# Scores of 32 queries at a time with the 288 keys they see, instead of 128 queries with 384

## The chip, the cores and the metric

One Trainium2 chip; the program runs on one of its cores. The time is what one execution takes on the device, in microseconds (us). A core has TensorE (PE; its weight loads are shown as PEld), VectorE (DVE), ScalarE (ACT), GpSimd (POOL) and a sync engine (SP) whose queue issues nearly all transfers here. Each engine works through its own instructions in order and waits for others by semaphores. Matmuls read SBUF, the on-chip memory of 128 partitions, and write PSUM, the accumulators.

## What is computed

One encoder layer over 4096 tokens of width 1024:

```python
proj = rmsnorm(x) @ w_in                      # q | k | v | g_a | u_p | g_p
s = q @ k.T * scale + bias                    # 8 query heads, 2 key heads of 64
s = where(abs(i - j) <= 128 and 0 <= j < 4096, s, -1e30)
m = max(max(s), sink)
p = exp(s - m) / (sum(exp(s - m)) + exp(sink - m))
a = (p @ v) * silu(g_a)
mixed = concat([a, pool(u_p) * silu(g_p)]) @ w_out
x = x + rmsnorm(mixed)
```

A query sees the keys at most 128 tokens away. For a block of 128 queries these lie in three blocks of keys, 384; for 32 queries in a row they lie in 128 + 32 + 128 = 288.

## The kernel before

Every float32 operand that goes through TensorE is held as a pair of float16 numbers, a high part and the rest, and a product of two is three matmuls (high x high, rest x high, high x rest).

The kernel has two parts. Up to about 498 us it prepares the weights and computes the gates and the pooling branch. After that comes the attention part, on which the change bears. It goes through 32 blocks of 128 queries from block 31 down to block 0, and each block in two halves of the heads (half 0 and half 1, four heads each). One such half block is a *visit*. Between the visits TensorE projects keys, values and queries of later blocks (`project_t`, `proj_v`; `aq`, `kv` in the profile) and multiplies finished blocks with the output weights (`product`, `last_product`; `m`, `ms`, `z`).

What follows for each visit, with the lines of the listing:

- `scores` (L1423): two PSUM tiles `s`, each for two heads. The two key heads lie in the upper and lower 64 partitions, so the matmuls of a pair use the upper and lower 64 rows of the array (64x128 each). A pair streams 384 keys; three pairs per tile for the float16 parts, 12 matmuls a visit. The keys lie in a ring of 1024 columns (`k_all`), and where the window goes over its end (blocks 7, 8, 15, 16, 23 and 24) each matmul is cut in two, 24 a visit.
- `logits` (L1444): one VectorE instruction a head adds the bias (with -1e30 where a key is masked) and takes the maximum, from PSUM to the float32 tile `p`. GpSimd writes the sink beside it (L1438).
- `exps` (L1455, ScalarE, in place, with the sum), `denominators` (L1462, L1465, VectorE), `probs` (L1477, ScalarE, high parts to `pn`), `rests` (L1485, VectorE, the rest to `pn`).
- `turn` (L1494): one transpose by DMA on SP's queue brings `pn`, queries on partitions, to `pt`, keys on partitions: 2 parts x 4 heads x 3 key blocks, 3072 columns.
- later, `values` (L1565): 36 matmuls for both halves of a block, the value heads in the left and right 64 columns of the array; then `gate` (L1573) on VectorE.

Blocks 31 and 0 are at the ends of the sequence and see only two key blocks: 256 columns in place of 384, and a transpose of 2048 columns.

The order of work on each engine is written out by hand. Every step is entered with a due time (`due(t, fn, ...)`; `visit`, `do_q`, `do_kv`, `attend` and the `mix_` functions set them), the list is sorted by these, and each engine executes its instructions in this order; the due times are no clock, only an order. After block 2 the steps to the end are listed one by one (`at_`, with `soft` for a softmax).

PSUM tiles `s` have two buffers, which is one visit; `p` and `pn` have two, `pt` three.

Of the kernel before, what the change touches and what calls it, by code (L numbers as in the profile page):

```python
# [17 lines left out]
P = 128  # L18
# [9 lines left out]
PN_BUFS = 2  # L28
# [40 lines left out]
def hybrid_layer(ctx: ExitStack, tc, io, out):  # L69
# [32 lines left out]
    bias = yflat[:, : NH * 3 * P].rearrange("p (h k) -> p h k", h=NH)  # L102
# [49 lines left out]
    with ExitStack() as actx:  # L152
# [423 lines left out]
        def small_loads():  # L576
            row_t["sk"] = pa1.tile([P, NH], F32, name="sk")
            nc.sync.dma_start(
                row_t["sk"], io["sink"].rearrange("(o a) -> o a", o=1).to_broadcast([P, NH])
            )  # L580
            nc.sync.dma_start(psc, io["pool_scale"])
            row_t["m"] = pa1.tile([P, 3 * P], F32, name="mask")
            nc.sync.dma_start(row_t["m"], io["mask"])

        def bias_load():

            f0 = f_scr[0:1, 0, :]
            for p0 in range(0, P, FR):
# [3 lines left out]
                        tensor=f0.tensor, offset=f0.offset + P - 1 - p0,  # L592
                        ap=[[NF - 1, FR], [(FR + 1) * NF, NH], [1, 3 * P]],
# [770 lines left out]
    k_all = pb1.tile([P, 2, RK], F16, name="k_all")  # L1364
    q_t, v_t = {}, {}
# [26 lines left out]
    pt, p_t, s_t, nm_t, den_t, rd_t, pn_t = {}, {}, {}, {}, {}, {}, {}  # L1392
# [12 lines left out]

    def scores(b, half):
        u, tl = divmod(b, 2)
        tl *= P
        kbs = keys(b)
        nk = len(kbs) * P  # L1410
        k0 = (b - 1 + kbs[0]) * P % RK
        cut = min(nk, RK - k0)
        segs = [(0, cut, k0)] + ([(cut, nk, 0)] if cut < nk else [])
        s_t[b, half] = []
        for jj in range(2):
# [3 lines left out]
            for n, (qi, ki) in enumerate(((0, 0), (1, 0), (0, 1))):  # L1419
                for c0, c1, kc in segs:  # L1420
                    for gg in range(2):
                        a = slice(64 * gg, 64 * gg + 64)
                        nc.tensor.matmul(  # L1423
                            s_ps[:, gg, c0:c1], q_t[u, half][a, qi, jj, tl : tl + P],
                            k_all[a, ki, kc : kc + c1 - c0], start=(n == 0 and c0 == 0),
                            stop=(n == 2 and c1 == nk), skip_group_check=True,
                        )

    def logits(b, half, i):

        kbs = keys(b)
        nk, lo, j0 = len(kbs) * P, kbs[0] * P, 2 * half
        if i == 0:
# [3 lines left out]
            p = p_t[b, half] = pb.tile([P, 4, 3 * P + 1], F32, name=f"p{b}_{half}", tag="p")  # L1437
            nc.gpsimd.tensor_copy(  # L1438
                p.rearrange("p (g j) k -> p g j k", g=2)[:, :, :, nk],
# [4 lines left out]
        nc.vector.tensor_tensor_reduce(  # L1444
            out=p_t[b, half][:, hh, :nk], in0=s_t[b, half][jj][:, gg, :nk],
            in1=bias[:, h, lo : lo + nk], scale=negc[:, h : h + 1], scalar=nsink[:, h : h + 1],
            op0=ALU.add, op1=ALU.min, accum_out=nm_t[b, half][:, hh : hh + 1],
        )

    def exps(b, half, i):  # L1450
        nk = len(keys(b)) * P
# [4 lines left out]
            p[:, hh, : nk + 1], p[:, hh, : nk + 1], AF.Exp, bias=nm_t[b, half][:, hh : hh + 1],  # L1456
# [9 lines left out]

    def prob_view(b, half):
        nk = len(keys(b)) * P
        return pn_t[b, half][:, : 8 * nk].rearrange("p (v h k) -> p v h k", v=2, h=4)

    def probs(b, half, i):
        nk = len(keys(b)) * P
        if i == 0:
            pn_t[b, half] = pb.tile(
                [P, 2 * 4 * 3 * P], F16, name=f"pn{b}_{half}", tag="pn", bufs=PN_BUFS
            )
        nc.scalar.activation(  # L1477
            prob_view(b, half)[:, 0, i], p_t[b, half][:, i, :nk], AF.Copy,
# [3 lines left out]
    def rests(b, half, i):  # L1482
        nk = len(keys(b)) * P
        pn4 = prob_view(b, half)
        nc.vector.scalar_tensor_tensor(  # L1485
            out=pn4[:, 1, i], in0=p_t[b, half][:, i, :nk], scalar=rd_t[b, half][:, i : i + 1],
# [3 lines left out]
    def turn(b, half):  # L1490
        kbs = keys(b)
        t = pb.tile([P, 2 * 4 * 3, P], F16, name=f"pt{b}_{half}", tag="pt", bufs=PT_BUFS)
        t4 = t[:, : 8 * len(kbs), :]
        nc.sync.dma_start(t4, pn_t[b, half][:, : 8 * len(kbs) * P], transpose=True)  # L1494
# [622 lines left out]
```

## Time and profile before

| | |
|---|---|
| median of 3 runs | 1189.21 us (1188.63 to 1189.54) |
| the profiled execution | 1190.11 us |
| span of its instructions | 1188.3 us |
| granted TensorE clock, mean | 0.999 of full speed |
| busy: TensorE, VectorE, ScalarE, GpSimd | 97%, 78%, 61%, 23% of the span |
| busy share of the 16 DMA engines by queue 1 | 71.2% |
| DMA packets | 304567, of which 213776 under 512 B |

The profile is of one execution. A row of a timeline reads: start, duration, engine, line, operation, what it writes and reads with the number of partitions and elements, how many in a row, and in brackets the idle time of the engine just before and what ended it. A row of grouped instructions has the busy time and the mean duration of one in ns, then the idle time before them. A row of the waits has who waited for whom, the total in us, how often, and the longest. A matmul's recorded duration goes beyond the time for which the array is taken, so records of successive matmuls overlap.

The costliest groups of the attention part that bear on the change (a program-wide count each):

| | instructions | busy us | mean ns |
|---|---|---|---|
| scores, PE L1423 | 912 | 73.1 | 296 |
| values, PE L1565 | 1128 | 68.1 | 274 |
| logits, DVE L1444 | 256 | 156.0 | 666 |
| rests, DVE L1485 | 256 | 156.7 | 659 |
| exps, ACT L1455 | 256 | 153.0 | 599 |
| probs, ACT L1477 | 256 | 136.3 | 596 |
| transposes pt, SP L1494 | 64 | | 6.1 us from issue to landing |

### The profile page before, as it was taken

To read this page: it belongs to the slowest core of one execution; us is meant where nothing else is said; L and a number is where in the kernel's file an instruction comes from. 1 tells how busy PE (TensorE), PEld (TensorE's weight loads), DVE (VectorE), ACT (ScalarE), POOL (GpSimd) and SP (SyncE) were. 2 spreads that over 40 slices of the span, in tenths; PEclk is the share of its full clock that TensorE was granted. 3 is DMA by queue.
4 is the path that set the end of the run, shared out by engine and by line. 5 is a ranking of instruction groups with operands and counts; after the bars stand their busy time and mean duration, and the time that the engine had idled before them with its cause. 6 is when DMAs were issued, how large, how long until landed. Compare 5 with 4: busy or idle time off the path is not lost. (4 is left out here: it accounts for less than half of the span.)

```text
span 1188.3 us, 25535 instructions
## 1 busy us (share of the span) xinstructions
PE 1156.1 (97%) x10180; PEld 848.3 (71%) x10180; DVE 930.4 (78%) x1780; ACT 719.3 (61%) x1593; POOL 271.5 (23%) x281
## 2 busy tenths in 40 slices
PE   5999999999999999899999999999999999999997
PEld 4548888888888888766576676666666657657643
DVE  5787887688888876767777877787787787787786
ACT  5756666557566443366575666667666566656672
POOL 1000000000000000012433532533443443353231
PEclk9999999999999999999999999999999999999999
DMA  9578796959788547788786676786576577566694
GB/s 258 148 239 241 197 269 149 320 119 305 156 292 193 163 164 204 255 236 209 194 196 125 188 196 151 169 200 172 143 204 178 120 201 195 127 189 161 145 251 124
DMA packets 304567, 230.08 MB, mean 194 GB/s; under 512 B 213776, under 2 KB 270736, under 8 KB 299456
## 3 DMA queue, kind: packets, MB, share of 16 engines
q1 hardware_dynamic: 304448, 228.45, 71.2%
q8 instruction: 79, 1.29, 0.4%
q14 instruction: 40, 0.33, 0.1%
HBM read 115.14 MB, written 62.44 MB: 149 GB/s over the span
## 5 line engine op out<-in xcount | busy, mean ns | idle before, releaser
L935 PEld LDWEIGHTS <-wa 128*128 128x128 f16 x3360 | 328.2, 98 | 41.8 <-issue 3.2
L935 PE MATMUL ch<-xt,wa 128*128 128x256 f16 x1920 | 212.3, 273 | 1.0 <-DVE u L960 1.0
L1386 PEld LDWEIGHTS <-raw 128*128 128x128 f16 x1920 | 185.2, 98 | 33.8 <-issue 9.7
L1455 ACT ACTIVATE p<-p,nm 128x385 f32<-128x385 f32 (+1 forms) x256 | 153.0, 599 | 57.1 <-POOL p L1438 37.9
L1485 DVE SCALAR_TENSOR_TENSOR pn<-p,rd,pn 128x384 f16<-128x384 f32 (+1 forms) x256 | 156.7, 659 | 26.0 <-ACT pn L1477 25.4
L1386 PE MATMUL aq<-xt,raw 128*128 128x256 f16 x1536 | 173.1, 273 | 0.0
L1697 PE MATMUL ms<-wo,ys 128*128 128x512 f16 x720 | 162.8, 379 | 1.6 <-ACT pn L1477 1.6
L1444 DVE CUSTOM_DVE_ANT_0 p<-s,ybig,nsink 128x384 f32<-128x384 f32 (+1 forms) x256 | 156.0, 666 | 1.3 <-PE s L1423 1.0
L1477 ACT ACTIVATE pn<-p,rd 128x384 f16<-128x384 f32 (+1 forms) x256 | 136.3, 596 | 23.6 <-ACT p L1455 22.1
L1697 PEld LDWEIGHTS <-ys 128*128 128x128 f16 x720 | 68.9, 98 | 84.7 <-issue 4.2
L1697 PE MATMUL m<-wo,y 128*128 128x512 f16 x540 | 119.7, 380 | 0.7 <-POOL y L1603 0.5
L935 PE MATMUL cl<-xt,wa 128*128 128x256 f16 x960 | 106.9, 273 | 1.8 <-DVE cbig L960 1.0
L1697 PEld LDWEIGHTS <-y 128*128 128x128 f16 x540 | 51.4, 98 | 65.5 <-issue 4.5
L296 DVE TENSOR_TENSOR xt<-ybig,xt 128x1024 f16<-128x1024 f32 x56 | 67.7, 1221 | 22.8 <-ACT xt L291 22.5
L1733 POOL TENSOR_TENSOR mo<-mo,ybig 128x512 f32<-128x512 f32 x39 | 64.9, 1665 | 87.0 <-ACT jkb L1722 85.8
L204 POOL TENSOR_SCALAR ssq<-ssq 128x4 f32<-128x4 f32 (+1 forms) x11 | 3.6, 329 | 345.8 <-ACT jk L195 339.7
L1462 DVE TENSOR_SCALAR den<-den 128x4 f32<-128x4 f32 x64 | 17.4, 272 | 76.6 <-ACT p L1455 76.5
L1423 PE MATMUL s<-k_all,q 64*128 64x384 f16 (+2 forms) x912 | 73.1, 296 | 2.8 <-ACT q L1376 1.4
L1565 PE MATMUL o<-pt,vv 128*64 128x256 f16 x1128 | 68.1, 274 | 1.8 <-DMA pt<-pn 1.8
L1565 PEld LDWEIGHTS <-vv 128*64 128x64 f16 x1128 | 59.1, 110 | 8.1 <-issue 6.7
L1423 PEld LDWEIGHTS <-q 64*128 64x128 f16 x912 | 36.9, 94 | 36.1 <-issue 12.6
L291 ACT CAST xt<-ybig 128x1024 f16<-128x1024 f32 x56 | 57.1, 1041 | 4.0 <-PE cl L935 2.1
(184 smaller groups left out, 1652.6 us busy)
## 6 DMA issues: line engine op xcount, KB each, us to landing
x_scr<-xt SPq DMA_DIRECT2D x16, 1024.0 KB, 4.4
xt<-x_scr SPq DMA_DIRECT2D x15, 1024.0 KB, 7.7
xn<-in_x SPq DMA_DIRECT2D x28, 512.0 KB, 7.5
ybig<-in_xT SPq DMA_DIRECT2D x28, 512.0 KB, 6.7
xr<-in_x SPq DMA_DIRECT2D x28, 512.0 KB, 4.0
out<-xr SPq DMA_DIRECT2D x28, 512.0 KB, 3.6
yp_scr<-yt SPq DMA_DIRECT2D x32, 256.0 KB, 2.6
raw<-in_w_out SPq DMA_DIRECT2D x16, 512.0 KB, 7.9
```

What stands on the lines that cost most here:

```text
L291: nc.scalar.copy(couple(m, c)[:, w, 0], y_view(i))
L296: eng.tensor_tensor(out=o[:, w, 1], in0=y_view(i), in1=o[:, w, 0], op=ALU.subtract)
L935: nc.tensor.matmul(acc[:, c], wa[:, q, wi, slot * HK + k, c * P : (c + 1) * P], x[:, xi, k, :], start=(fresh and n == 0), stop=(n > 3 * 2 ...
L1386: nc.tensor.matmul(acc, w[:, j, k, :], x[:, k // HK, a, k % HK, :], start=(n == 0), stop=(n == 3 * KT - 1),)
L1423: nc.tensor.matmul(s_ps[:, gg, c0:c1], q_t[u, half][a, qi, jj, tl : tl + P], k_all[a, ki, kc : kc + c1 - c0], start=(n == 0 and c0 == 0), ...
L1444: nc.vector.tensor_tensor_reduce(out=p_t[b, half][:, hh, :nk], in0=s_t[b, half][jj][:, gg, :nk], in1=bias[:, h, lo : lo + nk], scale=negc[ ...
L1455: nc.scalar.activation(p[:, hh, : nk + 1], p[:, hh, : nk + 1], AF.Exp, bias=nm_t[b, half][:, hh : hh + 1], scale=-1.0, accum_out=den_t[b, ...
L1477: nc.scalar.activation(prob_view(b, half)[:, 0, i], p_t[b, half][:, i, :nk], AF.Copy, scale=rd_t[b, half][:, i : i + 1],)
L1485: nc.vector.scalar_tensor_tensor(out=pn4[:, 1, i], in0=p_t[b, half][:, i, :nk], scalar=rd_t[b, half][:, i : i + 1], in1=pn4[:, 0, i], op0= ...
L1565: nc.tensor.matmul(o_ps[a, 2 * half : 2 * half + 2], v[:, vi, kt, a], pt[b, half][:, pi, g, :, i, :], start=(n == 0), stop=(n == last),)
L1697: nc.tensor.matmul(z_t[u, tag], y[:, k, yi, :], wo[o][:, wi, k, :], start=(n == 0 and acc is None), stop=(n == 3 * HK - 1), skip_group_che ...
L1733: eng.tensor_tensor(out=mo, in0=mo, in1=gpost[:, cs], op=ALU.mult)
```

## The change

Each group of 32 queries is scored with the 288 keys that it sees. The 128 queries of a block become four groups, each on 32 columns of the array: with the two key heads in the two row halves, eight tiles of 64x32. The group r reads the keys from column 32 r of the window on, and its scores stand in the same 288 columns of PSUM on its 32 partitions; bias and mask are laid out in the same way. The softmax instructions then go over 288 columns (289 with the sink) in place of 384.

```diff
+QR = 32
+NK = 2 * P + QR
+MG = 3 * P - NK
+BIG = 1e30
...
+    pn = [pb1.tile([P, MG + 8 * 3 * P], F16, name=f"pn{i}") for i in range(2)]
...
+    def seen(b, r):
+
+        return (P - QR * r if b == 0 else 0), (2 * P - QR * r if b == NB - 1 else NK)
...
             for n, (qi, ki) in enumerate(((0, 0), (1, 0), (0, 1))):
-                for c0, c1, kc in segs:
-                    for gg in range(2):
...
+                for r in range(P // QR):
+                    lo, hi = seen(b, r)
+                    k0 = ((b - 1) * P + QR * r + lo) % RK
+                    cut = min(hi, lo + RK - k0)
+                    rows = slice(QR * r, QR * r + QR)
+                    for c0, c1, kc in ((lo, cut, k0), (cut, hi, 0)):
+                        for gg in range(2 * (c1 > c0)):
+                            a = slice(64 * gg, 64 * gg + 64)
+                            nc.tensor.matmul(
+                                s_ps[rows, gg, c0:c1],
+                                q_t[u, half][a, qi, jj, tl + QR * r : tl + QR * r + QR],
+                                k_all[a, ki, kc : kc + c1 - c0], start=(n == 0 and c0 == lo),
+                                stop=(n == 2 and c1 == hi), skip_group_check=True,
+                            )
```

That makes 48 matmuls a visit in place of 12, and 96 in place of 24 where the ring wraps; each comes with its weight load. In all 3648 in place of 912.

In blocks 31 and 0 the groups see different columns (256, 224, 192 and 160 of them), so each head's logits are four VectorE instructions of 32 partitions; GpSimd first fills `p` with 1e30, which the exponential turns to zero:

```diff
+            if edge_block:
+                nc.gpsimd.memset(p[:, :, :NK], BIG)
...
+        for r in range(P // QR if edge_block else 1):
+            rows = slice(QR * r, QR * r + QR) if edge_block else slice(0, P)
+            lo, hi = seen(b, r)
+            nc.vector.tensor_tensor_reduce(
+                out=p_t[b, half][rows, hh, lo:hi], in0=s_t[b, half][jj][rows, gg, lo:hi],
...
```

The probabilities of a group stand 32 r columns further left than before. `pn` is now two fixed tiles, one for each half, in which every 288 columns are followed by 96 zeros, with 96 more zeros ahead of all (`margins`, GpSimd, once at the start). The transpose of a half block becomes four, one for each group of 32 queries, and each begins 32 r columns further left, so that `pt` has the same layout as before:

```diff
     def turn(b, half):
...
+        for r in range(P // QR):
+            c0 = MG - QR * r
+            nc.sync.dma_start(
+                t[:, :, QR * r : QR * r + QR],
+                pn[half][QR * r : QR * r + QR, c0 : c0 + 8 * 3 * P], transpose=True,
+            )
```

Blocks 31 and 0 now also transpose all three key blocks (3072 columns); `values` reads the two that exist. The due times of all steps stay; the order on each engine differs by the added instructions alone, and the values' first weight load and matmul of each half wait for the four transposes where one matmul waited for one.

More of the change, by code (lines that the diff above doesn't have):

```diff
@@ L1419, in scores @@
             for n, (qi, ki) in enumerate(((0, 0), (1, 0), (0, 1))):
-                for c0, c1, kc in segs:
-                    for gg in range(2):
[L1422 to L1427, printed above, removed]
+                for r in range(P // QR):
[12 more added lines that the diff above has]
+                            )
     def logits(b, half, i):
-        kbs = keys(b)
-        nk, lo, j0 = len(kbs) * P, kbs[0] * P, 2 * half
+        j0 = 2 * half
+        edge_block = b in (0, NB - 1)
         if i == 0:
```

63 lines of the change are left out of this document (26 added, 37 removed).

## The prediction

> **What bounds the kernel now.** I read the page first, then the busy time by stretches, then TensorE's waits.
>
> ```profile
> span 1188.3 us, 25535 instructions
> ...
> PE 1156.1 (97%) x10180; PEld 848.3 (71%) x10180; DVE 930.4 (78%) x1780; ACT 719.3 (61%) x1593; POOL 271.5 (23%) x281
> ```
> ```profile
> core 0: us, PE busy (x) PEld busy (x) DVE busy (x) ACT busy (x) POOL busy (x), PEclk, DMA share, GB/s
> 498.00:540.00 42.00, 37.90 (x380) 28.06 (x381) 27.78 (x77) 26.49 (x70) 4.66 (x7) 1.00 0.84 239
> 540.00:1118.00 578.00, 576.44 (x5175) 384.70 (x5174) 453.17 (x1009) 365.71 (x916) 234.05 (x228) 1.00 0.70 174
> 1118.00:1170.00 52.00, 51.01 (x346) 26.71 (x344) 46.09 (x107) 33.43 (x88) 14.55 (x16) 1.00 0.81 208
> ```
> ```profile
> PE o L1565 <- DMA pt<-pn: 1.8, 2, 1.1
> PE ms L1697 <- ACT pn L1477: 1.6, 1, 1.6
> PE s L1423 <- ACT q L1376: 1.4, 2, 0.8
> PE s L1423 <- DVE q L1377: 0.9, 2, 0.4
> ```
>
> The windows give busy time and instructions of each engine per stretch. The attention part starts at about 498 us. From 540 to 1118 TensorE (PE) is busy 576.44 of 578 us: every nanosecond taken from a matmul group there is a nanosecond of the kernel, and VectorE (453.17) and ScalarE (365.71) have room. The other two stretches differ. From 1118 to 1170 VectorE is busy 46.09 of 52 us, nearly as tight as TensorE. And around 498 to 540 TensorE waited for q (1.4 and 0.9 us), that is for the two engines that split the projection; a later VectorE shows there at once. So the middle is priced by matmuls, the ends by VectorE's chain.
>
> **The scores in the middle.** A visit (one block of 128 queries, one half of the heads) has 12 matmuls now, 24 where the ring of keys wraps (blocks 7, 8, 15, 16, 23, 24). The change makes 48, and 96 at a wrap; each brings its weight load.
>
> ```profile
> 840.08 1.16 PE L1423 MATMUL s<-k_all,q 64*128 64x256 f16 x24
> ...
> 851.64 1.15 PE L1423 MATMUL s<-k_all,q 64*128 64x384 f16 x12
> ...
> 858.09 2.15 PE L1565 MATMUL o<-pt,vv 128*64 128x256 f16 x36
> ```
> ```profile
> L1423 PE MATMUL s<-k_all,q 64*128 64x384 f16 x576 | 55.3, 324 | 0.5 <-ACT k_all L1376 0.5
> ...
> L1423 PE MATMUL s<-k_all,q 64*128 64x256 f16 x180 | 16.1, 270 | 1.2 <-ACT q L1376 0.7 <-DVE q L1377 0.4
> L1423 PE MATMUL s<-k_all,q 64*128 64x128 f16 x144 | 12.6, 217 | 0.0
> ```
>
> Columns: start, duration, matmuls; below, mean duration by shape. From 384 to 128 columns the mean falls by 107 ns, 0.42 ns a column. Of the visit at 851.64, 1.15 us less the last matmul's 0.324 leaves 0.826 us for five steps: 165 ns a step, what 384 columns stream. A step has two matmuls, so the two row halves run side by side; and the 36 value matmuls, (2.15 - 0.27) / 17 = 110 ns per pair for 256 columns, show that two column halves do too. If all eight tiles of the new visit do, a step is 288 columns, 165 - 96 x 0.42 = 125 ns; five steps and the shorter last matmul (40 ns) give 5 x 40 + 40 = 240 ns less per visit. That is the one bound. The other is the instructions' rate: 96 instructions in a visit, where the wrapped visit shows 48 in 1.16 - 0.27 = 0.89 us, 19 ns each, at no loss against the unwrapped one. At 19 ns the new visit would start its last matmul after 1.8 us, 1 us later than now. But 19 ns is what the columns asked for, not a limit that shows; I take 200 ns gained, near the good end. Visits: 64, less 12 wrapped and 4 of the edge blocks (whose columns, 256 at most, stay): 48 x 0.2 = **-9.6 us**.
>
> **The wrapped visits.** There a tile's columns come in two pieces, issued one behind the other on the same tile, and matmuls start in order, so the next tile's first piece stands behind this tile's second, which waits for this tile's first. In blocks 7, 15 and 23 the first pieces are 256, 224, 192 and 160 columns: a round costs 832 x 0.42 = 349 ns, six rounds 2.1 us, against 0.89 now: +1.2 us for each of 6 visits, **+7.2 us**. In blocks 8, 16 and 24 they are 128, 96, 64, 32, 134 ns a round, 0.8 us: nothing. Bounds: 0 if second pieces can overlap after all, and 192 instructions x 19 ns = 3.6 us, +2.7 us for 12 visits, 33 us.
>
> **The edge blocks.** For blocks 31 (first) and 0 (last) each head's logits become four VectorE instructions of 32 queries, with 256, 224, 192 and 160 columns.
>
> ```profile
> L1485 DVE SCALAR_TENSOR_TENSOR pn<-p,rd,pn 128x384 f16<-128x384 f32 x240 | 149.9, 671 | 23.0 <-ACT pn L1477 23.0
> L1444 DVE CUSTOM_DVE_ANT_0 p<-s,ybig,nsink 128x384 f32<-128x384 f32 x240 | 148.2, 674 | 0.3
> ...
> L1444 DVE CUSTOM_DVE_ANT_0 p<-s,ybig,nsink 128x256 f32<-128x256 f32 x16 | 7.8, 542 | 1.0 <-PE s L1423 1.0
> ```
> ```profile
> 499.65 0.54 DVE L1444 CUSTOM_DVE_ANT_0 p<-s,ybig,nsink 128x256 f32<-128x256 f32 x1 [0.49 <-PE s L1423]
> ...
> 500.12 0.54 DVE L1444 CUSTOM_DVE_ANT_0 p<-s,ybig,nsink 128x256 f32<-128x256 f32 x1
> ...
> 502.88 1.70 ACT L1477 ACTIVATE pn<-p,rd 128x256 f16<-128x256 f32 x4 [0.50 <-ACT p L1455]
> 503.42 1.68 DVE L1485 SCALAR_TENSOR_TENSOR pn<-p,rd,pn 128x256 f16<-128x256 f32 x4 [0.63 <-ACT pn L1477]
> ...
> 505.94 0.69 DVE L1377 SCALAR_TENSOR_TENSOR q<-aq,q 128x512 f16<-128x512 f32 x1 [0.85 <-ACT q L1376]
> ...
> 506.69 0.72 PE L1423 MATMUL s<-k_all,q 64*128 64x256 f16 x10 [0.44 <-DVE q L1377]
> 507.13 0.54 DVE L1444 CUSTOM_DVE_ANT_0 p<-s,ybig,nsink 128x256 f32<-128x256 f32 x1 [0.49 <-PE s L1423]
> ...
> 510.90 1.68 DVE L1485 SCALAR_TENSOR_TENSOR pn<-p,rd,pn 128x256 f16<-128x256 f32 x4 [0.64 <-ACT pn L1477]
> ...
> 513.27 0.42 DVE L1377 SCALAR_TENSOR_TENSOR k_all<-kv,k_all 128x256 f16<-128x256 f32 x1 [0.69 <-ACT k_all L1376]
> 513.29 1.29 PE L1423 MATMUL s<-k_all,q 64*128 64x384 f16 x12 [0.47 <-ACT k_all L1376]
> ```
>
> Logits start 0.47 us apart at 256 columns, and (674 - 542) / 128 = 1.03 ns a column: 0.47 + 0.44 + 0.40 + 0.37 = 1.68 us a head instead of 0.47, +1.2, **+4.8 us for four heads**; the quarter of the partitions saves nothing, since an instruction's time goes by columns (no row with 32 partitions shows it: 0 to 4.8, and I take 4.8). The 32 more columns of the other passes add 0.2. In block 31 this is on the path. The residual pass (503.42, 1.68 us) ends at 505.10, now 510.1; behind it on VectorE stands q's low part (505.94), which the matmuls at 506.69 wait for, and ScalarE's q stands behind its own late probabilities (502.88): TensorE comes 4.2 us later. The second half adds as much: its residuals, at 510.90 + 1.68, end at 512.6 + 4.2 + 5.0 = 521.8, and behind them is the low part of k (513.27), for which the matmuls of 513.29 wait. They have it at 522.2 instead of 513.7: **+8.5 us**, and from there on TensorE is full, so it stays.
>
> ```profile
> 1150.67 0.54 DVE L1444 CUSTOM_DVE_ANT_0 p<-s,ybig,nsink 128x256 f32<-128x256 f32 x1
> ...
> 1158.09 0.54 DVE L1444 CUSTOM_DVE_ANT_0 p<-s,ybig,nsink 128x256 f32<-128x256 f32 x1
> ...
> 1162.86 1.68 DVE L1485 SCALAR_TENSOR_TENSOR pn<-p,rd,pn 128x256 f16<-128x256 f32 x4 [1.15 <-ACT pn L1477]
> ...
> 1169.92 1.50 PE L1565 MATMUL o<-pt,vv 128*64 128x256 f16 x24
> ```
>
> Block 0 is alike: logits at 1150.67 and 1158.09, both +4.8. The residuals of the second half (1162.86 + 1.68 = 1164.5) end at 1174.4, the transposes land 5.5 us later (below) at 1179.9, where TensorE reached that half of the values 12 matmuls after 1169.92, at 1170.6: +9.3. The softmax passes of blocks 2 and 1 ahead of it, which VectorE's full queue puts on the path, lose 96 columns: 0.1 us an instruction, 0.4 for four logits and 0.4 for the residuals, one such chain: -0.8. Tail **+8.5 us**. The fill of the probability tile on GpSimd (4 x 288 columns, four times) comes where that engine is busy 4.66 of 42 and 14.55 of 52 us: nothing, or 1 to 2 us more if it were late.
>
> **The transposes.** One of 128 queries becomes four of 32, on SP's queue one behind the other.
>
> ```profile
> 852.17 3.68 SPq L1494 DMA_TRANSPOSE pt<-pn  x1
> ```
> ```profile
> DMA  0000000000000499999999999999477899930000
> ...
> DMA packets 3392, 1.31 MB, mean 131 GB/s; under 512 B 3136, under 2 KB 3136, under 8 KB 3392
> ```
> ```profile
> DMA to landing us min/median/max: 5.5/5.5/5.5
> ```
> ```profile
> DMA  0000000000000199999999999999999710000000
> ...
> DMA packets 2080, 0.52 MB, mean 95 GB/s; under 512 B 2080, under 2 KB 2080, under 8 KB 2080
> ```
>
> The edge transpose of 2048 columns moves 2080 packets in some 2.7 us (20 of the 40 slices of 0.1375 us), 1.3 ns each; the usual one has 3072 of the 3392 and lands 5.5 us after issue: about 1.5 us fixed, 4 us of packets. Four with 768 packets each, overlapped, land after 5.5 us again; taken wholly in turn, 4 x (1.5 + 1.0) = 10 us, +4.5. SP's queue is held 3.68 us by one now; plain transfers behind it are held up by whatever four hold more. I take the overlapped end: in the slices the two transfers that follow the transpose on the queue begin with no idle slice behind its last packets. What covers a longer one: the tightest transpose is the second of an odd block (852.17, landing 857.7), read from the 19th value matmul after 858.09, at 859.1 (half of 2.15): 1.4 us; and the softmax chain ahead is 0.8 us shorter. So nothing in the middle; the tail's 5.5 holds. The values' first instruction of each half now waits for four landings, and all of TensorE's queue stands behind it, as it stood behind one.
> [...] The fit above has 1.5 us, and no row shows whether four overlap.
>
> ScalarE and VectorE get lighter by some 0.07 to 0.1 us in each of four passes per head. In the middle that is worth nothing while TensorE is full. Margins of zero on GpSimd fall in the idle time before 498: nothing.
>
> **The sum.** -9.6 + 7.2 + 8.5 + 8.5 = +14.6 us, on the span of 1188.3: 1202.9. The profiled execution took 1190.1, 1.8 more than its span, 0.9 above the median of 1189.2; against the median I forecast **1204 us**. Its own range, with 0 to 240 ns per plain visit (-11.5 to 0) and wraps from 0 to twice the 7.2: 1195 to 1221.
>
> **Rivals.**
> 1. The instructions' rate binds. If a matmul and its load need 10 ns each, a plain visit issues for 0.96 us instead of 0.83 (+0.13 x 48 = 6) and a wrapped one for 1.9 (+1.0 x 12 = 12): with the 17 of the edges 1189 + 35 = 1224. At the full 19 ns, +48 and +33: 1287. For it: four times the instructions. Against: nothing shows a limit as high as 19. 15% for 1224, 5% for 1287 or beyond, where column quarters also would not overlap.
> [...]
> 2. The edges are covered, and the kernel is faster. Place: TensorE before blocks 31 and 0. VectorE is idle 14 of the 42 us from 498 to 540; if TensorE lost under 2.4 us at both ends together, the -9.6 and +7.2 would decide. With the ends at nothing and the full 240 ns: -11.5 + 7.2 = -4.3, 1185. Against: the queues' order is fixed and the q row above is already a wait. 10%.
> 3. The transposes go in turn, +4.5 us. Less 1.4 and 0.8 of cover, plus 0.4 by which TensorE gets there sooner: 2.7 us for each of 15 odd blocks, 40 us, and 4.5 in the tail: about 1248. For it: one queue, and no two transposes close together in the trace. Against: the slices without a gap, though these were plain transfers. 10%.
> The forecast keeps 60%.
>
> **How the numbers follow.** Faster, by over 0.2% (what a measurement here can tell from no change, 2.4 us): rival 2 with most of its 10%, and a little of the forecast's low end if wraps cost nothing: 0.10. Within 0.2%: 0.05. Slower: the rest, 0.85. The range goes from 1184, which takes in rival 2, to 1248: left out are the 5% at 1287, half of rival 3, and some 5% below or between.
>
> **What would show it.** Plain score visits of 0.9 us with 48 matmuls (right) or near 2 us (rival 1); visits of blocks 7, 15 and 23 above 2 us and those of 8, 16 and 24 near 1.1; VectorE with 16 logits in a row in blocks 31 and 0, TensorE idle some 4 us twice before 525 and 8 to 9 us before the values of block 0; transposes landing under 6.5 us after the first's issue, with no wait of the values on them in the middle. Wrong it would be if TensorE's idle time at the ends does not grow, or if the middle's matmul time grows by more than the wraps.

## The result, and the profile after

The changed kernel takes 1220.35 us (median of 4 runs, 1219.84 to 1221.54), the kernel before beside it 1189.38: ratio 1.026, 95% interval 1.0242 to 1.0278. It is 31 us slower; the forecast was 1204, 15 us slower. The profiled execution took 1219.84 us, 1.7 more than its span.

The page of the changed kernel, its span and the busy times:

```profile
span 1218.1 us, 31547 instructions
...
PE 1161.1 (95%) x12916; PEld 860.9 (71%) x12916; DVE 911.7 (75%) x1876; ACT 681.5 (56%) x1593; POOL 273.9 (22%) x289
```

The same kernel by stretches, as for the kernel before, followed by TensorE's waits (who for whom, us in all, times, longest):

```profile
core 0: us, PE busy (x) PEld busy (x) DVE busy (x) ACT busy (x) POOL busy (x), PEclk, DMA share, GB/s
496.00:526.00 30.00, 18.18 (x269) 13.78 (x270) 23.79 (x85) 10.91 (x31) 0.38 (x2) 0.77 0.71 219
526.00:566.00 40.00, 36.53 (x417) 25.35 (x414) 22.51 (x62) 22.28 (x60) 7.11 (x8) 0.87 0.69 134
566.00:1140.00 574.00, 567.87 (x7566) 389.46 (x7565) 412.01 (x1004) 327.24 (x910) 229.31 (x228) 1.00 0.82 174
1140.00:1218.00 78.00, 60.34 (x454) 28.70 (x451) 59.76 (x152) 30.54 (x83) 16.02 (x18) 0.90 0.65 163
```
```profile
PE o L1582 <- DMA pt<-pn: 12.3, 13, 3.2
PE s L1431 <- ACT q L1380: 7.1, 2, 6.3
PE s L1431 <- DVE nm L1458: 4.5, 2, 3.6
PE s L1431 <- ACT k_all L1380: 4.1, 1, 4.1
PE z L1686 <- ACT raw L1616: 3.4, 1, 3.4
```
```profile
PE o L1582 <- DMA pt<-pn: 9.1, 11, 3.2
```

TensorE executes more instructions, and its middle is no longer full: 567.87 of 574 us. At both ends it now stands idle for long (12 of 30 us from 496 to 526, 18 of 78 at the end, the last 6 of them behind its last matmul), and the granted clock there is 0.77 to 0.90, where the kernel before had 1.00 from 498 to 1170. Two kinds of waits have grown: the values wait for transposes 13 times, 12.3 us, in place of twice, 1.8 us (the last row: 11 of the 13, 9.1 us, stand in the middle from 540 to 1140), and the scores wait at the edges for q, for k and for the logits (`nm`), 16 us.

The visits, in a timeline of TensorE, a plain one and two wrapped ones (blocks 24 and 23):

```profile
659.77 1.19 PE L1431 MATMUL s<-k_all,q 64*32 64x128 f16 x96
...
671.56 1.26 PE L1431 MATMUL s<-k_all,q 64*32 64x256 f16 x96
```
```profile
867.06 0.93 PE L1431 MATMUL s<-k_all,q 64*32 64x288 f16 x48
```

A plain visit has 48 matmuls in 0.93 us, where it had 12 in 1.15; a wrapped one has 96 in 1.19 (block 24) and 1.26 (block 23), where the kernel before needed 1.16. All 12 wrapped visits take 1.17 to 1.27 us.

The first edge, in a timeline of all engines:

```profile
497.81 0.53 DVE L1458 CUSTOM_DVE_ANT_0 p<-s,ybig,nsink 32x256 f32<-32x256 f32 x1 [0.65 <-PE s L1431]
...
498.28 0.07 DVE L1458 DVE_READ_ACCUMULATOR2_ANT nm<- 32x1 f32 x1
498.37 0.50 DVE L1458 CUSTOM_DVE_ANT_0 p<-s,ybig,nsink 32x224 f32<-32x224 f32 x1
...
498.90 0.47 DVE L1458 CUSTOM_DVE_ANT_0 p<-s,ybig,nsink 32x192 f32<-32x192 f32 x1
...
499.39 0.46 DVE L1458 CUSTOM_DVE_ANT_0 p<-s,ybig,nsink 32x160 f32<-32x160 f32 x1
...
499.89 0.53 DVE L1458 CUSTOM_DVE_ANT_0 p<-s,ybig,nsink 32x256 f32<-32x256 f32 x1
...
509.61 0.39 PE L1431 MATMUL s<-k_all,q 64*32 64x256 f16 x8 [6.32 <-ACT q L1380]
...
510.41 1.25 PE L1431 MATMUL s<-k_all,q 64*32 64x256 f16 x40 [0.41 <-DVE q L1381]
...
511.59 4.79 PE L1390 MATMUL kv<-xt,raw 128*128 128x256 f16 x24
...
516.22 2.84 PE L1538 MATMUL kv<-raw,xt 128*128 128x128 f16 x48
...
523.15 1.92 PE L1431 MATMUL s<-k_all,q 64*32 64x288 f16 x48 [4.08 <-ACT k_all L1380]
525.00 7.53 PE L1390 MATMUL aq<-xt,raw 128*128 128x256 f16 x48
532.46 0.93 PE L1431 MATMUL s<-k_all,q 64*32 64x288 f16 x48
```

In the kernel before, the read of the accumulator and the next head's logits start at the same time (first row); the second row is the scores visit that stands at 532.46 above:

```profile
500.12 0.08 DVE L1444 DVE_READ_ACCUMULATOR2_ANT nm<- 128x1 f32 x1
...
519.85 1.15 PE L1423 MATMUL s<-k_all,q 64*128 64x384 f16 x12
```

Here a head's logits begin at 497.81, the next head's at 499.89: 2.08 us a head, where they were 0.47 apart. TensorE waits 6.32 us for q and 4.08 us for k; between the two waits its clock is halved (granted 0.50 from 505.5 to 515.7), and 24 matmuls of the kv projection take 4.79 us, which take 2.79 at the full clock (a run below). From 522.6 to 529.4 the clock is halved again (0.50): from the scores at 523.15 to the next at 532.46 it is 9.31 us, where the kernel before needs 6.56 (513.29 to 519.85).

The other edge, block 0, in the same view:

```profile
1164.73 0.42 DVE L1458 CUSTOM_DVE_ANT_0 p<-s,ybig,nsink 32x160 f32<-32x160 f32 x1
...
1179.12 19.32 SPq L1508 DMA_TRANSPOSE pt<-pn  x8
...
1189.22 1.03 PE L1686 MATMUL z<-wo,raw 128*128 128x512 f16 x2 [3.44 <-ACT raw L1616]
```
```profile
1197.52 0.85 PE L1582 MATMUL o<-pt,vv 128*64 128x256 f16 x12
1200.30 0.85 PE L1582 MATMUL o<-pt,vv 128*64 128x256 f16 x12 [1.93 <-DMA pt<-pn]
```

From block 0's first logits to its values 19.2 us have become 32.8 (1197.52 - 1164.73), and the values' second half waits for its transposes once more. The row of eight transposes is that of both halves: the second four can be issued only from 1192.12 on, behind their residuals, and the values that need them start at 1200.30, 8.2 us later.

### The profile page after: what moved, and what is told of

Same layout as the page of the kernel before. It is cut to its first block, busy times and chain, and to the rows that moved or that the text cites. A ratio compares the mean times of both kernels' runs of the same rounds, so it can differ in the third digit from the quotient of the medians.

```text
span 1218.1 us, 31547 instructions
## 1 busy us (share of the span) xinstructions
PE 1161.1 (95%) x12916; PEld 860.9 (71%) x12916; DVE 911.7 (75%) x1876; ACT 681.5 (56%) x1593; POOL 273.9 (22%) x289
## 4 chain that ended last, share of the span: by engine, by line
PE 78%; DMA 5%; DVE 5%; SPq 4%; issue 1%; ACT 1%; DVEq 0%; POOLq 0%; ACTq 0%
PE ch L938 16%; PE aq L1390 11%; PE ms L1714 11%; PE m L1714 9%; PE cl L938 8%; PE o L1582 5%; SPq L1508 4%; PE s L1431 4%; DMA pt<-pn 4%; PE pb L938 4%; PE a L888 3%; DVE p L1458 3%; PE kv L1390 2%; PE kv L1538 2%; PE pg L999 2%
## 5 line engine op out<-in xcount | busy, mean ns | idle before, releaser
L1390 PEld LDWEIGHTS <-raw 128*128 128x128 f16 x1920 | 187.7, 99 | 34.2 <-issue 7.0
L1469 ACT ACTIVATE p<-p,nm 128x289 f32<-128x289 f32 x256 | 134.3, 526 | 71.7 <-DVE nm L1458 36.0
L1458 DVE CUSTOM_DVE_ANT_0 p<-s,ybig,nsink 128x288 f32<-128x288 f32 (+4 forms) x304 | 155.6, 556 | 3.5 <-PE s L1431 2.0
L1499 DVE SCALAR_TENSOR_TENSOR pn<-p,rd,pn 128x288 f16<-128x288 f32 x256 | 133.0, 566 | 24.0 <-ACT pn L1492 18.8
L1492 ACT ACTIVATE pn<-p,rd 128x288 f16<-128x288 f32 x256 | 117.3, 523 | 26.9 <-issue 16.0
L1582 PE MATMUL o<-pt,vv 128*64 128x256 f16 x1128 | 73.6, 281 | 12.5 <-DMA pt<-pn 12.3
L299 DVE TENSOR_TENSOR xt<-ybig,xt 128x1024 f16<-128x1024 f32 x56 | 67.7, 1221 | 21.8 <-ACT xt L294 21.4
L1431 PE MATMUL s<-k_all,q 64*32 64x288 f16 (+7 forms) x3648 | 65.8, 270 | 16.5 <-ACT q L1380 7.1
L1476 DVE TENSOR_SCALAR den<-den 128x4 f32<-128x4 f32 x64 | 21.2, 331 | 76.7 <-ACT p L1469 76.7
L1582 PEld LDWEIGHTS <-vv 128*64 128x64 f16 x1128 | 60.4, 112 | 22.9 <-issue 20.7
L1431 PEld LDWEIGHTS <-q 64*32 64x32 f16 x3648 | 44.5, 92 | 38.4 <-issue 15.5
```

Source lines behind the costliest of these rows:

```text
L299: eng.tensor_tensor(out=o[:, w, 1], in0=y_view(i), in1=o[:, w, 0], op=ALU.subtract)
L1390: nc.tensor.matmul(acc, w[:, j, k, :], x[:, k // HK, a, k % HK, :], start=(n == 0), stop=(n == 3 * KT - 1),)
L1431: nc.tensor.matmul(s_ps[rows, gg, c0:c1], q_t[u, half][a, qi, jj, tl + QR * r : tl + QR * r + QR], k_all[a, ki, kc : kc + c1 - c0], start= ...
L1458: nc.vector.tensor_tensor_reduce(out=p_t[b, half][rows, hh, lo:hi], in0=s_t[b, half][jj][rows, gg, lo:hi], in1=bias[rows, h, lo:hi], scale ...
L1469: nc.scalar.activation(p[:, hh], p[:, hh], AF.Exp, bias=nm_t[b, half][:, hh : hh + 1], scale=-1.0, accum_out=den_t[b, half][:, hh : hh + 1],)
L1492: nc.scalar.activation(prob_view(b, half)[:, 0, i], p_t[b, half][:, i, :NK], AF.Copy, scale=rd_t[b, half][:, i : i + 1],)
```

## The experiments

Every run stands beside runs of the kernel before on the same chip (chips differ by up to 3.7 us), so ratios are compared.

| run | us | before | ratio (95%) |
|---|---|---|---|
| one_logits | 1198.38 | 1189.66 | 1.0075 (1.0046 to 1.0104) |
| before_logits4 | 1218.01 | 1189.66 | 1.0237 (1.0222 to 1.0252) |
| before_turn4 | 1212.06 | 1189.66 | 1.0189 (1.0172 to 1.0206) |
| after_turn1 | 1201.95 | 1189.66 | 1.0098 (1.0083 to 1.0113) |
| one_logits_turn1 | 1176.88 | 1190.94 | 0.9890 (0.9874 to 0.9907) |
| before_turncols4 | 1195.30 | 1192.89 | 1.0016 (1.0001 to 1.0031) |
| before_turn2 | 1204.65 | 1192.89 | 1.0103 (1.0080 to 1.0125) |
| before_turncols4r | 1202.31 | 1190.73 | 1.0093 (1.0074 to 1.0112) |
| after_filler | 1233.59 | 1192.89 | 1.0341 (1.0326 to 1.0357) |
| after_filler_o | 1220.58 | 1190.94 | 1.0258 (1.0242 to 1.0274) |
| scores8 | 1190.28 | 1192.89 | 0.9977 (0.9967 to 0.9986) |
| scores8_gain2 | 1189.78 | 1189.24 | 1.0010 (1.0000 to 1.0020) |
| before_gain2 | 1189.71 | 1189.24 | 1.0009 (1.0000 to 1.0018) |
| one_logits_order | 1189.19 | 1190.13 | 0.9991 (0.9978 to 1.0004) |
| one_logits_tail | 1186.01 | 1190.08 | 0.9969 (0.9956 to 0.9983) |

### The logits of the edge blocks

One part undone in the changed kernel (one_logits), and the same part alone put into the kernel before (before_logits4):

```diff
 # one_logits: scores(), blocks 31 and 0
+            if b in (0, NB - 1):
+                unseen = slice(0, P) if b == 0 else slice(2 * P - QR * (P // QR - 1), NK)
+                nc.vector.memset(s_ps[:, :, unseen], -BIG)
 # logits()
-        for r in range(P // QR if edge_block else 1):
...
+            out=p_t[b, half][:, hh, :NK], in0=s_t[b, half][jj][:, gg, :NK],
...
 # before_logits4: logits()
+        n4 = 4 if b in (0, NB - 1) else 1
+        for r in range(n4):
+            rows = slice(P // n4 * r, P // n4 * (r + 1))
```

> The changed kernel, but in blocks 31 and 0 the columns that a query does not see are filled with -1e30 in PSUM by one VectorE instruction per scores tile ahead of the matmuls, so that the logits of a head are one instruction over 288 columns again: 4 instead of 16 per half block, and no fill of p by GpSimd. Theory 1 (the four-part logits start the loss at both edges, and the idle TensorE's lower clock doubles it): most of the 32 us of the two edges goes, 1192 to 1200 us. Theory 2 (the edges lose by their four transposes, which land later than the one): 1212 to 1219 us. The forecast's own price of these logits (4.8 us per half block, about 5 us per edge on the path): 1208 to 1212 us.

> The kernel before with one part of the change: in blocks 31 and 0 the logits of a head are made in four VectorE instructions of 32 rows, over the same 256 columns; all else as before. Theory 1 (the logits start the edges' loss): 1189 plus 16 to 26, so 1205 to 1215 us, with the TensorE clock down for some us at both edges. Theory 2 (the transposes make it): 1189 plus at most 8, 1189 to 1197 us. The forecast's price: about 5 us per edge, 1197 to 1201 us.

Theory 1 holds for the logits, and the part alone costs more than it said: undoing the part saves 22.0 us, and the part alone costs the kernel before 28.4. What the lower clock has to do with it these two runs do not show. The two figures lie on both sides of the part's price: alone, all four instructions of a head go over 256 columns (some 2.24 us a head, an estimate from the 0.56 us between 497.81 and 498.37 above, against 2.08 in the changed kernel), and with the part undone TensorE waits for the fill that takes its place:

```profile
PE s L1434 <- DVE s L1424: 3.6, 2, 1.8
```

In the trace of before_logits4 TensorE's waits are those of the changed kernel, without those on transposes:

```profile
PE s L1423 <- ACT q L1376: 7.6, 2, 6.8
PE s L1423 <- DVE nm L1447: 6.1, 2, 4.1
PE s L1423 <- ACT k_all L1376: 4.9, 1, 4.9
PE z L1673 <- ACT raw L1603: 4.3, 1, 4.3
```

They are 22.9 us in all; the kernel before has 1.9 of them (q and k). ScalarE's q, k and `raw` casts stand behind its exponentials and probabilities, and these behind the logits.

### The transposes

Again one part alone (before_turn4) and one part undone (after_turn1):

```diff
 # before_turn4: turn()
-        nc.sync.dma_start(t4, pn_t[b, half][:, : 8 * len(kbs) * P], transpose=True)
+        for r in range(4):
+            rows = slice(32 * r, 32 * r + 32)
+            nc.sync.dma_start(t4[:, :, rows], pn_t[b, half][rows, : 8 * len(kbs) * P], transpose=True)
 # after_turn1: turn()
+        nc.sync.dma_start(t, pn[half][:, MG:], transpose=True)
```

> The kernel before with one part of the change: the transpose of each half block is issued as four of 32 rows each, without a shift; the bytes are the same. Theory (four short transposes land later than one, and odd blocks then wait for them in the middle): 9 to 19 us more, with waits of the values on the transposes between 540 and 1140 us that the kernel before does not have: 1198 to 1208 us. Rival (the forecast's: hidden in the middle): 1189 to 1193 us.

> The changed kernel with one transpose of 128 rows per half block instead of four shifted ones; the shift of each group of 32 queries is left out, so the values are those of other keys; the amount transposed is the same. Theory (the transposes give back the middle's gain, about 9 us, and 2 to 4 us at each edge): 1203 to 1209 us. Rival (the transposes are hidden in the middle, as forecast): 1216 to 1220 us.

The four transposes cost 22.4 us alone, and 18.4 us go when they are one again; both are more than expected, and "hidden in the middle" has fallen. Of this the changed kernel's trace shows 12.3 us as waits of the values on transposes; where the rest falls is not traced. In before_turn4 the values wait for transposes:

```profile
PE o L1569 <- DMA pt<-pn: 17.4, 19, 3.3
```

In the kernel before it was twice, 1.8 us. What a transpose of 32 rows does to the traffic shows in four views of the DMA engines, each of the same half block and over 11 us in 40 slices (busy tenths, then GB/s): the kernel before (one transpose), before_turn4 (four of 32 rows), and two runs told below, before_turn2 (two of 64 rows; GB/s alone) and before_turncols4r (four of 128 rows):

```profile
DMA  0000000039999999999999568999500000000200
GB/s 0 0 0 0 0 0 0 0 61 230 216 204 219 217 222 219 214 217 215 221 221 173 154 164 283 350 387 387 194 0 0 0 0 0 0 0 0 60 0 0
```
```profile
DMA  0000000008999649998389994699960159999102
GB/s 0 0 0 0 0 0 0 0 5 159 165 145 138 101 84 176 160 154 122 60 134 168 152 145 79 116 172 152 157 107 10 67 201 424 387 380 380 67 0 60
```
```profile
GB/s 0 0 0 0 0 0 57 179 159 142 153 150 144 142 136 90 57 153 140 155 155 157 154 157 154 134 135 62 52 380 380 380 424 179 7 0 60 0 0 0
```
```profile
DMA  0000000008995089951999429992984999810000
GB/s 0 0 0 0 0 0 0 0 0 179 218 211 107 7 182 210 214 102 12 203 210 211 79 44 215 214 204 39 104 112 156 387 372 417 313 45 0 0 0 0
```

(Above 280 GB/s at the end are plain transfers behind them.) One transpose runs at 204 to 230 GB/s without a break, until its last slices. Four of 32 rows run mostly at 138 to 176, with dips to between 60 and 84; two of 64 rows at much the same rate (134 to 159), with one dip to 57; four of 128 rows at over 200, with gaps of 7 to 44. So is it the number or the shape?

```diff
 # before_turncols4: turn(); before_turncols4r has reversed(range(4)); before_turn2 has two of 64 rows
+        for r in range(4):
+            n = 2 * len(kbs)
+            nc.sync.dma_start(t4[:, n * r : n * r + n],
+                pn_t[b, half][:, n * r * P : (n * r + n) * P], transpose=True)
```

> The kernel before, the transpose of each half block issued as four, split by columns: each has all 128 rows and a quarter of the columns; the same bytes and the same number of transposes as in the run split by rows (1212 us). Theory A (each transpose costs its own start on SP and a gap between them, whatever its shape): 1205 to 1214 us. Theory B (a transpose of only 32 rows moves at half the rate): 1189 to 1195 us.

> The kernel before, the transpose of each half block issued as two of 64 rows each. Theory A (a fixed cost for each transpose: one more instead of three more): about a third of 22 us, 1194 to 1199 us. Theory B (the rate falls with the rows): 1200 to 1206 us if 64 rows run at an intermediate rate, 1189 to 1192 us if only 32 rows are slow.

> The kernel before with four transposes by columns, the last quarter first: it holds the last head's residuals, so that no transpose can start before the residual pass ends, as with the split by rows. (In the first order the quarters of the high parts were issued 1.7 us before that end, by the trace, so that run did not tell the shape from the number.) Theory A (four starts cost it, whatever the shape): 1206 to 1212 us, as by rows. Theory B (a transpose of 32 rows moves its packets at a lower rate, 150 instead of 215 GB/s in the trace): clearly less, 1192 to 1202 us, since only the gaps between the four are left.

The first run seemed to say "shape": 2.4 us. But its first two quarters hold only high parts and were issued before the residuals were made, so it had a start that the split by rows has not. With the last quarter first the same four cost 11.6 us, at the upper edge of what theory B allowed. So number and shape each stand for about half of the 22: the gaps between four starts some 11, the lower rate of 32 rows the rest, by difference. Two of 64 rows (11.8 us), with one gap, already pay the lower rate.

Both parts undone at once:

> The changed kernel with both costs taken out at once: the edge blocks' logits in one instruction per head (the columns not seen filled with -1e30), and one unshifted transpose per half block (the shift of the groups of 32 queries is left out, so the values are those of other keys). What is left of the change: the scores on eight tiles and the softmax over 288 columns. Theory (the costs add: 1220 minus 22 minus 18, and the score visits' 0.22 us come out whole because VectorE is lighter too): 1178 to 1182 us. Rival (another loss stands behind these two): 1186 us and above.

```diff
 # one_logits with turn() of after_turn1
```

1176.88 us, a little under the theory's range: 43.5 less than the changed kernel, 3 more than the two savings together (22.0 and 18.4), and 14 less than the kernel before beside it. This is what the eight tiles and the shorter softmax are worth, wrapped visits included.

### The halved clock

> The changed kernel with matmuls that nothing reads (224 columns each, into the unused columns of a score tile) put where TensorE waits longest at the edges: 50 ahead of the scores of block 31's second half, 28 after the kv projection behind it, 25 within the scores of block 0's second half and 25 ahead of the first product of the last unit. They hold TensorE busy in the four long waits. Theory (the halved clock after these waits is a part of the edges' cost of its own): the clock stays at 1.0 there and 6 to 12 us go, 1208 to 1214 us. Rival (the path at the edges runs through ScalarE and VectorE, the clock costs nothing): 1219 to 1223 us.

```diff
+    def filler(n, tile, u, half, k0):      # matmuls that nothing reads
 # in the plan, at the waits
+            pe(2.5, filler, 46, u, 0, 3 * UT)   # after_filler_o, into the bank of the values
```

This first form did not test it: the filling matmuls wrote into score tiles and so waited themselves for the logits. A row of the waits says so (L1442 is the filler's line):

```profile
PE s L1442 <- DVE nm L1467: 17.1, 4, 7.5
```

The second form writes into the bank of the values, which waits for nothing there:

> The changed kernel again with matmuls that nothing reads, now into the bank of the values, which is free at these places: 46 of 256 columns ahead of the scores of block 31's second half, 28 behind the kv projection that follows, 26 ahead of the second score tile of block 0's second half. They depend on nothing late, so they can run at once within the waits (6.3, 4.1 and 3.6 us). Theory (the halved clock is a cost of its own): no half clock from 500 to 535 us, and from the end of the q projection to the first values of block 31 the time falls from 47.8 us (31.7 in the kernel before) to 41 to 44; the total 1212 to 1217 us. Rival (the edges' path runs through VectorE and ScalarE alone): 47 us or more there, and 1219 to 1223 us.

```profile
503.59 5.19 PE L1443 MATMUL fill<-k_all,q 128*128 128x256 f16 x46
...
510.89 0.72 PE L1433 MATMUL s<-k_all,q 64*32 64x256 f16 x40 [0.52 <-DVE q L1381]
511.54 2.79 PE L1390 MATMUL kv<-xt,raw 128*128 128x256 f16 x24
...
516.85 3.22 PE L1443 MATMUL fill<-k_all,q 128*128 128x256 f16 x28
523.41 1.92 PE L1433 MATMUL s<-k_all,q 64*32 64x288 f16 x48 [3.34 <-ACT k_all L1380]
```

The clock stays up: the scores take 0.72 us and the kv matmuls 2.79, not 1.25 and 4.79. The kv projection ends at 517.01 (514.17 + 2.84), not at 519.06 (516.22 + 2.84), though the run is 0.5 us late, and then TensorE meets k at 523.41 (523.15 in the changed kernel). From the end of the q projection to the values of block 30's second half (551.41) it is 47.7 us, where the changed kernel had 47.8. The total is the same. By the clock records of the two traces the changed kernel is at half clock five times before its last matmul, from 505.5, 522.6, 549.9, 1171.1 and 1188.2, some 37.6 us in all; here only the stretches from 522.7 and 1188.3 are left, 13.6 us. The halved clock from 505.5 is a consequence of the wait and no cost of its own; the theory has fallen for it, and nothing is won by the other two that went. The two that are left stay open. The one from 522.6 looks like a cost: the 9.31 us in place of 6.56 above lie between block 30's two score visits, and 18.6 us behind the second of them (at 551.06) the values wait for that visit's transposes.

### The scores alone, and the values behind other work

> The kernel before with one part of the change: the scores alone on eight tiles of 32 queries by 288 keys, each written at its place among the 384 columns, so that softmax (384 columns), the bias and the single transpose stay as they were; the columns a group of queries does not see keep old scores, which the bias masks. The two score tiles are held for the whole stage and filled once with zeros. Theory (0.2 us per visit, wrapped visits cost nothing more, nothing else on the path): 1189 minus 10 to 12, 1177 to 1181 us. Rival (the forecast's 1.2 us for six wrapped visits): 1184 to 1188 us. Rival (the rate of the 48 short matmuls binds): 1189 us and above.

```diff
 # scores8: scores(); softmax, bias and transpose as before
+                for r in range(4):
+                    lo, hi = max(32 * r, e0), min(32 * r + 2 * P + 32, e0 + len(kbs) * P)
...
+                                s_ps[rows, gg, c0 - e0 : c1 - e0],
```

The kernel gains 2.6 us, not 10, though each plain visit is 0.22 us shorter in the trace. Another engine ends the wait now:

```profile
PE aq L1387 <- DVE mo L1731: 4.3, 13, 0.5
PE o L1569 <- DMA pt<-pn: 2.4, 3, 1.2
```

Thirteen times the q projection waits for an accumulator that VectorE empties (`gain11`, `mo`) behind the residual pass over 384 columns. Moving that one instruction ahead was tried.

> The run with the scores alone on eight tiles, and one VectorE instruction of each unit moved: the multiplication by the gain that empties the accumulator of the next q projection goes ahead of the residual pass (3 us earlier in the plan), into an idle time of VectorE. Theory (in the run before this, TensorE got to that projection 0.44 us ahead of VectorE, 13 times, and some waits on transposes ate the rest): 4 to 7 us less than that run, a ratio of 0.992 to 0.995 to the kernel before, some 1181 us. Rival (the wait only moves to the residuals and the transposes behind them): ratio 0.997 to 1.000.

> The kernel before with only the move of that VectorE instruction, as a control. Theory (TensorE does not wait there in the kernel before): no change, ratio 0.999 to 1.001. Rival (the move is worth something by itself): ratio 0.998 or less.

In scores8_gain and before_gain (1249.38 and 1255.20 us) it stood ahead of the product as well and multiplied what the accumulator held before, so these two show only that the product then waits for it 14 times (47.5 and 45.0 us). Behind the product's issue it reads what it should:

> The scores alone on eight tiles, and the gain multiplication of each unit moved on VectorE from behind the residual pass to behind its first instruction, after the product that it reads (0.1 us behind the product's end in the plan became the time of its issue). Theory (TensorE reached the next q projection 0.44 us before VectorE had emptied its accumulator, 13 times in the run without the move): those 13 waits go, the ratio to the kernel before is 0.992 to 0.995, some 1181 to 1184 us. Rival (the wait moves to the residuals and the transposes behind them): 0.997 to 1.000.

> The kernel before with only that move, as a control. Theory (TensorE does not wait there in the kernel before, so nothing is won): ratio 0.999 to 1.001. Rival (the move is worth something without the eight tiles): 0.997 or less.

```diff
-        due(t + 0.1, gain11, u)
+        due(t - M + 0.02, gain11, u)
```

The rival holds: the 13 waits are gone and others have come, and no time is won. The values' waits on transposes go from 2.4 to 4.7 us, and 2.1 us are on accumulators that VectorE empties (`mo`); these do not make up all of the 10 us. So the 14 us of one_logits_turn1 need the softmax over 288 columns too. That VectorE and ScalarE follow TensorE too closely with 384 is read from these waits; the shorter softmax was not run alone.

What keeps one_logits above 1177 are 23 us of waits on transposes. In it the values were put behind work that does not wait:

```diff
 # one_logits_order, odd blocks
-            attend(b + 1)
             visit(b, 1)
+            attend(b + 1)
 # one_logits_tail, besides: values of blocks 2 and 1 behind the step after them, the fill of s earlier
+    at_(11.5, scores, 1, 1)
+    at_(12.6, values, 2)
```

> The changed kernel with the edge blocks' logits in one instruction per head (1198 us), and the values of the block before put behind the second score visit of each odd block instead of ahead of it, in block 29 behind the kv projection too, so that 0.9 us (there 6.5 us) of other matmuls stand between the transposes' issue and the values that wait for them. Theory (what is left above 1177 us are waits of the values on transposes of 32 rows, most of them under 1.5 us each and one of 7.2 us in block 29): 1185 to 1191 us, with the waits on the transposes down from 23 to under 10 us. Rival (the values' followers, gate and sums, are then late in turn, or the next block's transposes are late as well): 1195 to 1200 us.

> The run with the moved values (1189 us), with two more places covered: in the tail the values of blocks 2 and 1 also go behind the work that stood after them (the second scores of block 1, and one product), with the gate of block 1 behind the logits; and the fill of the unseen score columns stands earlier on VectorE, so that the first scores of the edge blocks do not wait for it. Theory (the remaining waits on the transposes, 1.7 and 2.8 us, and about 1.7 us of waits on the fill go, 6 us together): 1182 to 1185 us, faster than both kernels. Rival (the tail's path runs through the softmax of block 0, which the moved values only displace): 1187 to 1191 us.

The waits on transposes fall from 23.2 to 6.8 and 3.7 us:

```profile
PE o L1578 <- DMA pt<-pn: 23.2, 15, 7.2
```
```profile
PE o L1578 <- DMA pt<-pn: 6.8, 5, 2.8
```
```profile
PE o L1582 <- DMA pt<-pn: 3.7, 4, 2.4
```

The first is level with the kernel before, the second 0.31% faster (0.17 to 0.44%) and some 34 us faster than the changed kernel. Its median is 1 us above what was expected. So most of these were waits at places of the order, not a chain that any order pays.

## Why the prediction was right or wrong

The direction was right, and so was the softmax's chain as what binds at the ends; the middle that stays full of TensorE was not. The forecast was 16 us too low: 15 us slower, where 31 were measured. Two steps failed low (the transposes, put at nothing, and the edges) and one high (the wrapped visits). The forecast's own range, to 1221, takes in 1220.35 by luck: its upper end stood for wrapped visits at twice their price, and these cost nothing.

- **Plain visits, -9.6 us: right.** 0.93 us against 1.15 is 0.22 each, 10.6 us in all. That they come out whole depends on the shorter softmax: alone they bring 2.6. Of the lighter ScalarE and VectorE the prediction said "in the middle that is worth nothing while TensorE is full"; this failed.
- **Wrapped visits, +7.2 us: wrong, it is nothing.** "The next tile's first piece stands behind this tile's second, which waits for this tile's first" was the author's assumption, in no row of before, and does not happen: 1.26 us against 1.16 in block 23. Without the edges' logits and the four transposes the change is at -14 us, which leaves no room for this term. Over all 12 wrapped visits the rows show 0 to 0.11 us each, under 1 us together.
- **Edge logits, +4.8 us per half block and +8.5 per edge: the mechanism right, the size too small.** A head takes 2.08 us, not 1.68, so four heads +6.4. The sum counted the starts 0.47 us apart that the row of before shows. There the next logits start together with the read of the accumulator, at 500.12; here they start behind it (498.28 + 0.07, then 498.37), so the four are 0.56, 0.53, 0.49 and 0.50 us apart; why, no run shows. That the quarter of the rows saves nothing was right (0.53 us for 32 rows of 256 columns, 0.54 for 128). From the first logits to the scores of block 30 it was 513.29 - 499.65 = 13.6 us and is 523.15 - 497.81 = 25.3: +11.7 in place of +8.5. "From there on TensorE is full, so it stays" left out the halved clock, which adds 2.8 us up to 532.46 in the trace. In block 0 the values come 13.5 us later against their logits, and their second half, for which the sum had 9.3, 15.6 (35.6 us behind the first logits, in place of 19.9); there the four transposes take 8.2 us, where the sum kept 5.5. The edges' logits cost 22 to 28 us by the runs, not 17.
- **Transposes, nothing in the middle: wrong.** "Four with 768 packets each, overlapped, land after 5.5 us again" failed: the slices show dips between the four and, for 32 rows, mostly 138 to 176 GB/s in place of about 215. The plain transfers that followed the transpose without a gap were no evidence for transposes. The cost is 18 to 22 us, the rival's 40 was too high: the waits in the changed kernel are 0.3 to 3 us each.
- **The halved clock** is not in the prediction at all. The stretch from 505.5 costs nothing; the one from 522.6 stays open.
- **The sum:** by the runs that changed one part, 22 to 28 for the edges' logits and 18 to 22 for the transposes, less 13 for the rest (the ratio of 0.989 with both taken out), is 27 to 37, and 31 was measured; the prediction had 17 + 0 - 9.6 + 7.2. Of the 13 the score visits are 10.6; what makes up the other 2 to 3 was not run apart.

In its own list of what would show it, "TensorE idle some 4 us twice" came out as 6.3 and 4.1, "8 to 9 us before the values of block 0" as 7.9 (the waits for `nm` and `raw`), "visits of blocks 7, 15 and 23 above 2 us" as 1.26, "transposes landing under 6.5 us after the first's issue" as 8.2 in block 0, and "no wait of the values on them in the middle" as 11 of the 13 waits.

## What to carry to other kernels

Splitting a VectorE instruction by rows of the partition dimension saved no time here (0.53 us for 32 rows, 0.54 for 128, at 256 columns; 2.08 us a head in place of 0.47), and splitting a transpose by rows lowered its rate (from about 215 to about 150 GB/s) and left gaps. So price a split at the full cost of each piece plus the overlap that the pieces lose, and look for a way to keep one instruction: here a fill of the unseen columns. A shift that has to be made by four transposes should be planned with their later landing (in block 0 the values start 8.2 us after the issue), by putting work that waits for nothing between issue and use. A gain on the busiest engine can be eaten up by waits for the next one, as in the run with the scores alone (2.6 us won, where the visits are 10.6 shorter): price the second engine's distance at every place where the first is to come earlier.

## What the runs showed of the hardware

- Matmuls of 64x32 array tiles overlap: 48 of 288 columns take 0.93 us (the mean record of one is 0.291). In the wrapped visits, with second pieces on the same tile, 96 take 1.17 to 1.27 us, 24 of 64x128 in the kernel before 1.16 and 1.17.
- A VectorE instruction of 32 rows takes what one of 128 rows takes (0.53 and 0.54 us at 256 columns). Where four of 32 rows follow one another, the next starts behind the read of the accumulator before it (498.37, the read ends at 498.35); of 128 rows it starts with the read (500.12).
- In the half block shown, a DMA transpose of 32 or 64 rows runs at about 150 GB/s, one of 128 rows at about 215; four of 128 rows in a row leave gaps of 7 to 44 GB/s, four of 32 rows dips to between 60 and 84.
- TensorE's clock fell to half in waits of 3 to 6 us and stayed there for 7 to 10 (in the changed kernel from 505.5 to 515.7 and four times more before its last matmul); a wait of 3.30 us at 551 in after_filler_o did not lower it. Filling the wait of 6.3 us with matmuls kept it up, at no gain.
